# One weight unit of an expert layer is loaded in two transfers, and a scatter waits for four stores without a memset before it

## The chip, the cores and the metric

One Trainium2 chip, one of its cores. The metric is the device time of one launch in microseconds (us). The kernel before took 933.2 us, the median of three runs (932.6 to 933.7).

## The reference

One layer of a bidirectional encoder over 512 tokens of width 1024: three attention branches in parallel, their gated sum, a layer norm, an expert-choice mixture of 16 experts, and a second layer norm. The change lies in the last two steps. Cut to what matters there:

```python
aff = softmax(x @ w_router)
gate, idx = top_k(aff.T, 64)                     # each of 16 experts takes 64 tokens
h = einsum('becd,edf->becf', x[idx], w_gate_up)  # w_gate_up: 16 x 1024 x 2048
hg, hu = split(h, 2)
ye = einsum('becf,efd->becd', silu(hg) * hu, w_down) * gate
x = layer_norm(alpha * x + zeros.at[idx].add(ye))
```

## The kernel before, in words

Everything is float32. An expert's weights are cut into 12 units of 1 MB: eight of gate and up ("gu", e, k), 128 rows of 2048 numbers each, and four of down ("dn", e, k). All 192 units lie one behind the other in `in_wx`, in the order in which they are used. `_blocks` (line 50) lists the loads: pairs of units as one transfer of 2 MB, or single units of 1 MB at the start and at the end. `Ring.load` (line 885) issues the next one on SyncE's queue (line 920) into a ring of SBUF buffers; `Ring.done` calls it as soon as TensorE has read what lay in the buffer. Row r of a unit goes to partition r. A unit of 128 rows is spread over all 16 DMA engines, eight rows each.

TensorE works through the experts in order. `gate_up` (L1408) multiplies the 64 gathered tokens of an expert with a unit (16 matmuls, L1421), `act_h` makes the activation, `down` (L1467, L1475) multiplies it with the four down units one expert later. The results are added to the tokens' rows with one-hot matmuls (`combine`, L1558), between the units of later experts.

The last expert is dealt with apart. While its gate and up units run, the second layer norm is finished for all 512 rows without it, and four stores of 512 KB each (`norm_bias` L1638 for three, `norm_end` L1645 for the last) write the output on SyncE's queue, behind the last weights. `last_down` (L1672) then works out the 64 rows that the last expert touches anew: 128 matmuls of 128 columns (L1683), one quarter for each down unit, then statistics on VectorE (L1694 to L1697), the normalised rows `ul` (L1700, L1701), and an indirect DMA from GpSimd (L1703) that overwrites these rows in the output. It may not run before the four stores have landed. For that a memset of one number in each tile of `XO` (L1702) stands ahead of it on GpSimd: it writes the tile that the stores read, so it waits until they have landed, and the scatter comes behind it on the same engine.

Of the kernel before, what the change touches and what calls it, by code (L numbers as in the profile page):

```python
# [18 lines left out]
P = 128  # L19
# [15 lines left out]
N_SINGLE = 18  # L35
FULL = 43
EXTRA = ("gu", 1, 2)
X_SCALE = 1024.0
A_SCALE = 16384.0


def lead(e):
    return {NEXP - 2: 2, NEXP - 1: 1}.get(e, 4)
# [6 lines left out]
def _blocks():  # L50
    order = []
    for e in range(NEXP):
        order += [("gu", e, k) for k in range(lead(e))]
        if e:
            order += [("dn", e - 1, k) for k in range(4)]
        order += [("gu", e, k) for k in range(lead(e), KD)]
    order += [("dn", NEXP - 1, k) for k in range(4)]
    order.remove(EXTRA)
    blocks, i, r = [], 0, 0
    while i < len(order):  # L60
        for tag, n in RING:
            left = ROUNDS.get(tag, len(order)) - r
            if left > 0 and i < len(order):
                keys = order[i:i + n]
                i += n
                if r and (i < FULL or i > len(order) - N_SINGLE):
                    blocks += [(tag, h, [key]) for h, key in enumerate(keys)]
                else:
                    blocks.append((tag, 0, keys))
        if r == 0:  # L70
            tags = [t for t, _, _ in blocks]
            blocks.insert(tags.index("M"), ("Z", 0, [EXTRA]))
            blocks.insert(tags.index("raw") + 1, ("X", 0, order[i:i + 1]))
            i += 1
        r += 1
    return blocks
# [3 lines left out]
def layer_kernel(ctx: ExitStack, tc: tile.TileContext, xt, xn, first0, wu, bgate, rpb, gains, wrt,  # L80
                 lnp, lnt, wx, csn, nmask, tri, iota, out, dbg=None):
    nc = tc.nc
# [218 lines left out]
    gT = cp.tile([P, KD], F32, name="gT")  # L301
    nc.gpsimd.tensor_scalar(gT, lnT[:, 0], 1.0 / X_SCALE, None, op0=ALU.mult)

# [573 lines left out]
    class Ring:  # L877
# [7 lines left out]
        def load(self):  # L885
            tag, h, keys = self.blocks[self.n]
            n = len(keys)
            src = wx[self.row:self.row + P * n].rearrange("(p j) (h c) -> p (j h) c", j=n, h=2)
            if tag == "X":
                key, = keys  # L890
                spare["bf"] = R("bf", [P, 768], "wxa")
                g = [spare["bf"][:, :512], R("tmp", [P, 512], "wxb", bufs=2)]
                u = R("gb", [P, D], "wxc")
                nc.sync.dma_start(u, src[:, 1])
                nc.sync.dma_start(g[1], src[:, 0, 512:])
                nc.sync.dma_start(g[0], src[:, 0, :512])
                self.t[key] = [g, u]
                self.at[key] = (tag, 0)
                self.row += P
                self.n += 1  # L900
                return
            if tag == "Z":
                key, = keys
                spare["xs"] = R("hi", [P, 2, KD, 2 * CAP], "xs")
                g = spare["xs"][:, 1].rearrange("p k c -> p (k c)")
                u = [spare["bf"][:, 512:], small([P, 5 * CAP], "same", bufs=1)[:, :256],
                     spare["x1T"].rearrange("p a s -> p (a s)")]
                nc.sync.dma_start(g, src[:, 0])
                nc.sync.dma_start(u[0], src[:, 1, :256])
                nc.sync.dma_start(u[1], src[:, 1, 256:512])  # L910
                nc.sync.dma_start(u[2], src[:, 1, 512:])
                self.t[key] = [g, [u[:2], u[2]]]
                self.at[key] = (tag, 0)
                self.row += P
                self.n += 1
                return
            if tag not in self.home:
                self.home[tag] = R(tag, [P, 2 * dict(RING)[tag], D], f"w{self.n}")
            full = self.home[tag][:, 2 * h:2 * (h + n)]
            nc.sync.dma_start(full, src)  # L920
            for j, key in enumerate(keys):
                t = [full[:, 2 * j + i] for i in range(2)]
                if key[0] == "dn" and key[1] == NEXP - 1:
                    t = [x.rearrange("p (c n) -> p c n", c=4) for x in t]
                self.t[key] = t
                self.at[key] = (tag, h + j)
                self.busy.add((tag, h + j))
            self.row += P * n
            self.n += 1
# [254 lines left out]
    def norm_cols(ms):  # L1184
        c = slice(ms[0], ms[-1] + 1)
        nc.gpsimd.tensor_scalar(r13[:, c], rs_y[:, c], X_SCALE, None, op0=ALU.mult)
        for m in ms:
# [358 lines left out]
    def residual_rows(h):  # L1546
        g, b = (ln_row(i, h, f"r1{i}{h}")[:, None, :].to_broadcast([P, 2, 512]) for i in range(2))
        for mp in range(2):
            a = acc_half(mp, h)
            nc.vector.scalar_tensor_tensor(a, a, DN_ALPHA / X_SCALE, g, op0=ALU.mult, op1=ALU.mult)  # L1550
        for mp in range(2):
# [58 lines left out]
        for o in range(2):  # L1610
            nc.vector.tensor_copy(idx[o * 64:o * 64 + 64], ix[o * 64:o * 64 + 64, o:o + 1])

    XO = []

    def norm_mean(m):
        if m == 0:
            XO.append(R(ring.free_at_end.pop(0), [P, NT, D], "xo"))
        c = slice(m, m + 1)
        nc.gpsimd.tensor_scalar(l2_n[:, c], l2_s[:, m, 0:1], l2_s[:, m, 1:2], -1.0 / D, op0=ALU.add, op1=ALU.mult)
        nc.scalar.activation(XO[0][:, m], acc_of(m), AF.Square, bias=l2_n[:, c], accum_out=l2_q[:, c])  # L1620

# [5 lines left out]
    def norm_gain(m):  # L1627
        for o in range(2):
            c = slice(o * 512, o * 512 + 512)
            nc.vector.scalar_tensor_tensor(XO[0][:, m, c], acc_of(m)[:, c], l2_n[:, m:m + 1], LATE["g"][o], op0=ALU.add,  # L1630
                                           op1=ALU.mult)

    def norm_scale(m):
        nc.scalar.activation(XO[0][:, m], XO[0][:, m], AF.Copy, scale=l2_y[:, m:m + 1])

    def norm_bias(m):
        nc.gpsimd.tensor_tensor(XO[0][:, m], XO[0][:, m], LATE["b"], op=ALU.add)
        nc.sync.dma_start(out[:, m], XO[0][:, m])  # L1638

    def norm_end(m):  # L1640
        for o in range(2):
            c = slice(o * 512, o * 512 + 512)
            nc.vector.scalar_tensor_tensor(XO[0][:, m, c], XO[0][:, m, c], l2_y[:, m:m + 1], LATE["b"][:, c], op0=ALU.mult,
                                           op1=ALU.add)
        nc.sync.dma_start(out[:, m], XO[0][:, m])  # L1645

    def last_rows(zb):
        for m in range(NT):
# [23 lines left out]
    def last_down(zb, h, banks):  # L1672
        st = LATE["sl"]
        hT = R("bf", [P, 4, P], "hTl")
        w = {}

        def part(q, i):
            if q not in w:
                w[q] = [x[:, c] for x in ring.get("dn", NEXP - 1, q) for c in range(4)]
            for j in range(4 * i, 4 * i + 4):  # L1680
                c, hf = divmod(j, 2)
                for o in range(2):
                    nc.tensor.matmul(zb[o * 64:o * 64 + 64, q * P:(q + 1) * P], hT[:, c, hf * 64:hf * 64 + 64],  # L1683
                                     w[q][4 * hf + c][:, o * P:(o + 1) * P], start=False, stop=(q == 3 and j == 7))
            if i:
                ring.done("dn", NEXP - 1, q)

        last_transpose(hT, h, 0, banks[0])
        last_own(zb, 1)
        part(0, 0)  # L1690
        last_transpose(hT, h, 1, banks[1])
        for q, i in ((1, 0), (0, 1), (1, 1), (2, 0), (2, 1), (3, 0), (3, 1)):
            part(q, i)
        nc.vector.bn_stats(st[:, 0], zb)  # L1694
        for i in (0, 64):
            nc.vector.tensor_tensor(st[64 - i:P - i, 1], st[i:i + 64, 0], st[i:i + 64, 2], op=ALU.add)
        nc.vector.bn_aggr(sl_mv, st[:, :2])  # L1697
        nc.gpsimd.tensor_tensor(sl_y, sl_mv[:, 1:2], power[:, :1], op=ALU.pow)
        u = R("t", [P, 512], "ul", bufs=2)
        nc.vector.scalar_tensor_tensor(u, zb, sl_mv[:, 0:1], LATE["gh"], op0=ALU.subtract, op1=ALU.mult)  # L1700
        nc.vector.scalar_tensor_tensor(u, u, sl_y, LATE["bh"], op0=ALU.mult, op1=ALU.add)  # L1701
        nc.gpsimd.memset(XO[0][:1, :, :1], 0.0)  # L1702
        nc.gpsimd.indirect_dma_start(out.rearrange("p m (o c) -> (p m o) c", o=2),  # L1703
                                     bass.IndirectOffsetOnAxis(ap=idx, axis=0), u, None)

    onehot(0, 0, 2)
    g0 = gather(0, 0, 2)
# [124 lines left out]
def _expert_rows(wgu, wdn):  # L1832
    import numpy as np
    dn = _down_slots(wdn)
    unit = {"gu": lambda e, k: wgu[e, k * P:(k + 1) * P], "dn": lambda e, k: dn[e, k]}
    return np.concatenate([np.stack([unit[t](e, k) for t, e, k in keys], 1).reshape(-1, 2048) for _, _, keys in _blocks()])


def _norm_rows(g1, b1, g2, b2):
# [106 lines left out]
```

## Time and profile before

| what | value |
|---|---|
| median of three runs | 933.2 us |
| the profiled execution | 932.51 us |
| its span, first to last instruction | 930.7 us |
| TensorE busy | 916.6 us (98%) |
| TensorE's granted clock, mean | 0.997 of full speed |
| moved by DMA | 251.41 MB |

The span is what the profile shows; 1.8 us of the profiled execution lie around it. A matmul's end is modelled, so TensorE's busy share does not say that it never waits: its waits are read from the weight loads (PEld), which stand one ahead of the matmuls. A "DMA share" of 1.0 means that all 16 DMA engines of the core are busy all the time.

### The profile page before, as it was taken

How to read it: one execution, taken by the hardware profiler on the slowest of the kernel's cores; microseconds unless marked ns; L12 is line 12 of the kernel's file. 1: busy time of each engine (PE TensorE's matmuls, PEld its weight loads, DVE VectorE, ACT ScalarE, POOL GpSimd, SP SyncE). 2: the span in 40 equal slices, each digit the busy share in tenths (PEclk: the TensorE clock that was granted, in tenths of full speed). 3: DMA queues.
4: the chain of work that ended last, by engine and by line, in shares of the span. 5: the costliest groups of instructions: out<-in, count | busy, mean ns of one | idle time of the engine just before them, and what ended most of it. 6: DMA issues, size and time to landing. Idle time of an engine off the chain costs nothing.

```text
span 930.7 us, 12821 instructions
## 1 busy us (share of the span) xinstructions
PE 916.6 (98%) x5216; PEld 591.5 (64%) x5216; DVE 438.9 (47%) x797; ACT 298.7 (32%) x568; POOL 90.3 (10%) x113
## 2 busy tenths in 40 slices
PE   9999999999999999999999999999999999999896
PEld 8898888888888888888776343444344334433334
DVE  6457958664476576338454112563232222331244
ACT  6345465665444454334232112111111111111022
POOL 0001304000122230100032000000000000000014
PEclk9999999999999999999999999999999999999998
DMA  9320221120432332566939999999999999999996
GB/s 366 124 92 23 91 73 64 46 90 25 119 99 102 106 85 69 193 260 247 413 123 406 426 429 430 430 428 431 431 429 431 430 431 430 431 431 428 427 425 290
DMA packets 40570, 251.41 MB, mean 270 GB/s; under 512 B 13168, under 2 KB 13808, under 8 KB 25536
## 3 DMA queue, kind: packets, MB, share of 16 engines
q1 hardware_dynamic: 40432, 250.34, 66.9%
q8 instruction: 41, 0.67, 0.3%
q0 software_dynamic: 80, 0.26, 0.1%
q14 instruction: 17, 0.14, 0.0%
HBM read 247.44 MB, written 2.36 MB: 268 GB/s over the span
## 4 chain that ended last, share of the span: by engine, by line
PE 87%; DMA 5%; DVE 4%; ACT 3%; issue 1%; POOL 0%; POOLq 0%; ACTq 0%; DVEq 0%; SPq 0%
PE g L1421 11%; PE u L1421 11%; PE y L1475 10%; PE gate L308 4%; PE gate L310 4%; PE gate L309 4%; DMA w<-in_wx 4%; PE ga L1378 3%; PE cb L1558 3%; PE pr L308 2%; PE pr L309 2%; PE pr L310 2%; PE nqk L310 2%; PE nqk L309 2%; PE nqk L308 2%; ACT att_twin L681 1%
## 5 line engine op out<-in xcount | busy, mean ns | idle before, releaser
L1421 PE MATMUL g<-w,xs 128*64 128x512 f32 x504 | 131.3, 599 | 1.3 <-DMA w<-in_wx 1.2
L1421 PE MATMUL u<-w,xs 128*64 128x512 f32 x504 | 129.5, 592 | 0.0
L1475 PE MATMUL y<-w,hT 128*64 128x512 f32 x480 | 106.0, 593 | 1.5 <-DMA w<-in_wx 1.2
L108 DVE TENSOR_TENSOR y<-y,y 64x512 fp32r<-64x512 f32 x30 | 20.7, 689 | 167.2 <-ACT y L107 167.2
L1421 PEld LDWEIGHTS u<-w,xs 128*64 128x64 f32 x504 | 36.2, 137 | 72.0 <-issue 71.1
L1475 PEld LDWEIGHTS y<-w,hT 128*64 128x64 f32 x480 | 34.2, 137 | 70.2 <-issue 65.4
L310 PE MATMUL gate<-xh,los 128*128 128x512 f32 x192 | 74.8, 389 | 0.0
L1421 PEld LDWEIGHTS g<-w,xs 128*64 128x64 f32 x504 | 32.9, 136 | 60.8 <-issue 54.6
L108 DVE TENSOR_TENSOR los<-raw_twin,his 128x1024 fp32r<-128x1024 f32 x38 | 50.6, 1336 | 39.4 <-ACT his L107 39.2
L107 ACT CAST y<-y 64x512 fp32r<-64x512 f32 x30 | 17.4, 579 | 141.5 <-PE y L1475 130.2
L308 PE MATMUL gate<-xh,his 128*128 128x512 f32 x144 | 56.9, 395 | 0.0
L309 PE MATMUL gate<-xl,his 128*128 128x512 f32 x144 | 56.1, 390 | 0.0
L1567 DVE TENSOR_TENSOR acc<-acc,cb 128x512 f32<-128x512 f32 x50 | 31.1, 682 | 37.7 <-PE cb L1558 37.7
L107 ACT CAST his<-raw_twin 128x1024 fp32r<-128x1024 f32 x39 | 40.8, 1046 | 5.3 <-PE wo L1213 2.0
L310 PEld LDWEIGHTS gate<-xh,los 128*128 128x128 f32 x192 | 36.0, 188 | 7.6
L1378 PEld LDWEIGHTS <-xhl 128*128 128x128 f16 x448 | 27.9, 98 | 8.0 <-issue 7.1
L681 ACT ACTIVATE att_twin<-gs,nm 128x512 f32<-128x512 f32 x32 | 21.7, 684 | 34.3 <-DVE nm L680 34.3
L1378 PE MATMUL ga<-oh,xhl 128*128 128x128 f16 (+1 forms) x448 | 30.6, 227 | 0.2
L308 PEld LDWEIGHTS gate<-xh,his 128*128 128x128 f32 x144 | 27.0, 188 | 5.8 <-DVE macc L556 0.2
L108 DVE TENSOR_TENSOR los<-raw_twin,los 128x1024 fp32r<-128x1024 f32 x20 | 25.3, 1263 | 11.4 <-ACT los L107 11.3
L309 PEld LDWEIGHTS gate<-xl,his 128*128 128x128 f32 x144 | 27.1, 188 | 5.3
L1465 ACT COPY hT<-ht 128x512 f32<-128x512 f32 x12 | 7.0, 586 | 72.6 <-PE ht L1460 72.6
(474 smaller groups left out, 1750.4 us busy)
## 6 DMA issues: line engine op xcount, KB each, us to landing
w<-in_wx SPq DMA_DIRECT2D x75, 2048.0 KB
w<-in_wx SPq DMA_DIRECT2D x40, 1024.0 KB
raw_twin<-in_wu SPq DMA_DIRECT2D x65, 512.0 KB
raw<-in_wu SPq DMA_DIRECT2D x8, 512.0 KB
xr<-in_xt SPq DMA_DIRECT2D x4, 512.0 KB
macc<-in_xn SPq DMA_DIRECT2D x2, 1024.0 KB
out<-xo SPq DMA_DIRECT2D x4, 512.0 KB
first<-in_first SPq DMA_DIRECT2D x4, 384.0 KB
```

The source lines that it names most:

```text
L107: nc.scalar.copy(hi, src)
L108: nc.vector.tensor_tensor(lo, src, hi.bitcast(F32), op=ALU.subtract)
L308: nc.tensor.matmul(acc, w_h, rh[:, k], start=(k == 0), stop=False)
L309: nc.tensor.matmul(acc, w_h, rl[:, k], start=False, stop=False)
L310: nc.tensor.matmul(acc, w_l, rh[:, k], start=False, stop=(k == nk - 1))
L681: nc.scalar.activation(self.p[:, h], self.s[h], AF.Exp, bias=nm[:, h:h + 1], accum_out=self.sm[:, h:h + 1])
L1378: nc.tensor.matmul(g, x[:, m, c], oh[:, m, sl], start=(m == 0 and x is XH), stop=(m == NT - 1 and x is XL))
L1421: nc.tensor.matmul(GU[e][b][hf * 64:hf * 64 + 64, c:c + n], xs, x, start=(k == 0), stop=(k == KD - 1))
L1465: nc.scalar.copy(homes[0][:, c], (tq if c.start else tp)[:, c])
L1475: nc.tensor.matmul(y[o * 64:o * 64 + 64], hT[:, c, hf * 64:hf * 64 + 64], w[j][:, o * 512:(o + 1) * 512], start=(k == 0 and j == 0), stop= ...
L1558: nc.tensor.matmul(cb, GT[pr][:, m], part[:, c], start=(n == 0), stop=(n == len(parts) - 1))
L1567: nc.vector.tensor_tensor(a, a, cb, op=ALU.add)
```

## The change

It takes one unit, ("gu", 6, 1), the second gate and up unit of expert 6, out of its pair, so that the block list has two loads of 1 MB there in place of one of 2 MB. The unit itself is loaded with two transfers: rows 0 to 79 as before, and rows 80 to 127 with a source of three dimensions, six groups of eight rows. For this the host lays those 48 rows out in another order, so that six groups are interleaved and can't be merged into one run. The destination of each row is the partition that it had before. The diff's own word for the number of groups is `LOW`, six; a transfer with an outer dimension of six is worked on by six DMA engines, eight rows each, and the transfer of 80 rows by sixteen, five rows each.

In the tail the memset goes, and the scatter gets a dependency on each of the four stores.

```diff
+APART = ("gu", 6, 1)
+LOW = 6
...
-                if r and (i < FULL or i > len(order) - N_SINGLE):
+                if r and (i < FULL or APART in keys or i > len(order) - N_SINGLE):
...
-            nc.sync.dma_start(full, src)
+            if keys == [APART]:
+                m = P - 8 * LOW
+                nc.sync.dma_start(full[:m].rearrange("p j c -> p (j c)"), wx[self.row:self.row + m])
+                nc.sync.dma_start(full[m:].rearrange("p j c -> p (j c)"),
+                                  wx[self.row + m:self.row + P].rearrange("(b a) c -> a b c", a=LOW))
+            else:
+                nc.sync.dma_start(full, src)
...
-        nc.sync.dma_start(out[:, m], XO[0][:, m])
+        STORES.append(nc.sync.dma_start(out[:, m], XO[0][:, m]))
...
-        nc.gpsimd.memset(XO[0][:1, :, :1], 0.0)
-        nc.gpsimd.indirect_dma_start(out.rearrange("p m (o c) -> (p m o) c", o=2),
+        put = nc.gpsimd.indirect_dma_start(out.rearrange("p m (o c) -> (p m o) c", o=2),
                                      bass.IndirectOffsetOnAxis(ap=idx, axis=0), u, None)
+        for x in STORES:
+            tc.add_manual_dep(put.ins, x.ins.name, mybir.DependencyInfo(mybir.DependencyClass.Sync, mybir.DependencyReason.DATA),
+                              reason="the same rows of the output")
...
+    rows = [np.stack([unit[t](e, k) for t, e, k in keys], 1).reshape(-1, 2048) for _, _, keys in _blocks()]
+    i = next(i for i, b in enumerate(_blocks()) if b[2] == [APART])
+    m = P - 8 * LOW
+    rows[i] = np.concatenate([rows[i][:m], rows[i][m:].reshape(LOW, 8, 2048).swapaxes(0, 1).reshape(-1, 2048)])
+    return np.concatenate(rows)
```

## Rows read from the trace of the kernel before

**Rows 1.** The page: the span, TensorE's busy share, DMA share in 40 slices.

```profile
span 930.7 us, 12821 instructions
...
PE   9999999999999999999999999999999999999896
...
DMA  9320221120432332566939999999999999999996
```

**Rows 2.** DMA view from 500 to 926 us: queue and kind, packets, MB, share of 16 engines.

```profile
DMA packets 16056, 181.33 MB, mean 426 GB/s; under 512 B 1803, under 2 KB 2046, under 8 KB 2720
...
q1 hardware_dynamic: 16032, 180.98, 99.8%
q8 instruction: 19, 0.31, 0.3%
```

**Rows 3.** Waits of PEld from 500 us on: total us, times, longest.

```profile
PEld g L1421 <- DMA w<-in_wx: 3.5, 5, 2.1
...
PEld y L1475 <- DMA w<-in_wx: 3.2, 3, 2.1
```

**Rows 4.** Timeline of PEld: a usual weight load, and those behind the waits.

```profile
862.94 0.14 PEld L1475 LDWEIGHTS y<-w,hT 128*64 128x64 f32 x2 [0.28 <-issue]
863.90 0.20 PEld L1475 LDWEIGHTS y<-w,hT 128*64 128x64 f32 x4 [0.82 <-DMA w<-in_wx]
...
868.74 0.20 PEld L1475 LDWEIGHTS y<-w,hT 128*64 128x64 f32 x4 [2.07 <-DMA w<-in_wx]
...
873.59 0.20 PEld L1421 LDWEIGHTS g<-w,xs 128*64 128x64 f32 x4 [2.08 <-DMA w<-in_wx]
...
910.88 0.24 PEld L1421 LDWEIGHTS g<-w,xs 128*64 128x64 f32 x4 [0.61 <-DMA w<-in_wx]
```

**Rows 5.** Chain of waits: the weight load and the last store in it.

```profile
837.56 35.99 DMA w<-in_wx
...
917.79 7.80 DMA out<-xo
925.58 0.02 issue
925.61 0.04 POOLq L1702
925.65 0.07 issue
925.72 0.09 POOL xo L1702
925.81 0.46 issue
926.27 1.47 POOLq L1941
```

**Rows 6.** Stretches of the tail: engines' busy time, PEclk, DMA share, GB/s (last three).

```profile
919.00:920.00 1.00, 1.00 (x22) 1.00 (x20) 0.00 (x0) 0.00 (x0) 0.00 (x0) 1.00 1.01 414
920.00:920.50 0.50, 0.50 (x14) 0.48 (x10) 0.00 (x0) 0.00 (x0) 0.00 (x0) 1.00 0.94 385
...
922.00:922.50 0.50, 0.50 (x12) 0.32 (x6) 0.00 (x0) 0.00 (x0) 0.00 (x0) 1.00 0.50 205
...
924.50:925.00 0.50, 0.00 (x0) 0.00 (x0) 0.40 (x2) 0.00 (x0) 0.05 (x1) 0.90 0.24 98
925.00:925.50 0.50, 0.00 (x0) 0.00 (x0) 0.50 (x1) 0.00 (x0) 0.00 (x0) 0.50 0.02 8
...
920.50:925.50 5.00, 2.06 (x37) 1.73 (x32) 2.66 (x6) 0.00 (x0) 0.55 (x1) 0.94 0.48 193
```

**Rows 7.** Stretches around the time of the unit's load.

```profile
610.00:620.00 10.00, 10.00 (x46) 3.85 (x42) 9.22 (x11) 0.60 (x1) 0.00 (x0) 1.00 1.02 433
620.00:630.00 10.00, 10.00 (x51) 4.45 (x52) 3.69 (x7) 1.17 (x2) 0.00 (x0) 1.00 1.00 428
630.00:640.00 10.00, 10.00 (x68) 4.16 (x65) 1.80 (x4) 1.62 (x3) 0.00 (x0) 1.00 1.00 428
```

**Rows 8.** Timeline of SyncE's queue: the loads issued from 608 us on, merged.

```profile
608.69 23.32 SPq L920 DMA_DIRECT2D w<-in_wx  x6
```

**Rows 9.** Line 920: duration of a load's issue on SyncE, min/median/max ns, count.

```profile
L920 SPq DMA_DIRECT2D w<-in_wx x115: 327/328/1392, 383.4 to 900.8; - x115
```

**Rows 10.** Timeline, all engines: the matmuls of the last down units and what follows.

```profile
916.13 6.43 PE L1683 MATMUL end<-w,hTl 128*64 128x128 f32 x112
...
922.61 0.70 DVE L1694 BATCH_NORM_STATS2 late<-end 128x6 f32<-128x512 f32 x1 [4.89 <-PE end L1683]
...
924.81 0.75 DVE L1701 SCALAR_TENSOR_TENSOR ul<-ul,sly,late 128x512 f32<-128x512 f32 x1
925.72 0.09 POOL L1702 MEMSET xo<- 1x4 f32 x1 [1.17 <-DMA out<-xo]
926.52 1.22 POOL L1703 DMA_INDIRECT out<-ul,idx  x1 [0.71 <-issue]
```

**Rows 11.** Stretches of two copies of 64 partitions each, lines 520 and 521.

```profile
237.50:238.00 0.50, 0.50 (x4) 0.42 (x3) 0.00 (x0) 0.50 (x1) 0.00 (x0) 1.00 1.05 430
...
238.50:239.00 0.50, 0.50 (x4) 0.42 (x3) 0.50 (x1) 0.00 (x0) 0.00 (x0) 1.00 1.09 221
239.00:239.50 0.50, 0.50 (x4) 0.42 (x3) 0.36 (x1) 0.00 (x0) 0.00 (x0) 1.00 0.88 197
```

More of the change, by code (lines that the diff above doesn't have):

```diff
@@ L1611, in slot_tables @@
             nc.vector.tensor_copy(idx[o * 64:o * 64 + 64], ix[o * 64:o * 64 + 64, o:o + 1])
-    XO = []
+    XO, STORES = [], []
     def norm_mean(m):
@@ L1644, in norm_end @@
                                            op1=ALU.add)
-        nc.sync.dma_start(out[:, m], XO[0][:, m])
+        STORES.append(nc.sync.dma_start(out[:, m], XO[0][:, m]))
     def last_rows(zb):
@@ L1835, in _expert_rows @@
     unit = {"gu": lambda e, k: wgu[e, k * P:(k + 1) * P], "dn": lambda e, k: dn[e, k]}
-    return np.concatenate([np.stack([unit[t](e, k) for t, e, k in keys], 1).reshape(-1, 2048) for _, _, keys in _blocks()])
+    rows = [np.stack([unit[t](e, k) for t, e, k in keys], 1).reshape(-1, 2048) for _, _, keys in _blocks()]
[3 more added lines that the diff above has]
+    return np.concatenate(rows)
 def _norm_rows(g1, b1, g2, b2):
```

## The prediction

> **What bounds the kernel now.** I began with the page's slices. TensorE is busy throughout, and from the 19th slice on so is DMA [rows 1]. The DMA view of that part alone says how full: 181.33 MB from 500 to 926 us at 426 GB/s, the sixteen engines taken up to 99.8% by loads and stores and to 0.3% by instruction fetches, 19 of them [rows 2]. So the mixture of experts runs at the speed of the weights, as long as TensorE waits for them. It does: PEld waits 3.5 and 3.2 us in all [rows 3], and the timeline puts the long waits late: 0.82 us before 863.90, 2.07 before 868.74, 2.08 before 873.59, 0.61 before 910.88, against 0.28 that a usual load idles [rows 4]. Up to 860 us TensorE lives off what the ring holds; behind that each unit's landing sets its pace. The chain agrees: the load that frees TensorE at 873.60 was issued 35.99 us earlier [rows 5], so SyncE is far ahead and only the queues' drain counts.
>
> A transfer has landed when the last of its engines has. The tail shows how unlike the engines are: the rate is 414 GB/s up to 920, then falls in steps to 205 at 922.00 and 98 at 924.50, and only in the half microsecond from 925.00 it is near nothing [rows 6]. No more loads are queued then, so each step is an engine running dry. The first is done about 920.2, the last about 925.0. From 920.5 to 925.5 the engines move 5.00 × 193 = 0.97 MB, which sixteen at 430 GB/s would move in 2.2 us [rows 6]. So the last engine ends some 2.5 us after a perfectly even split would (920.5 + 2.2 = 922.7 against about 925.2).
>
> **The change, part by part.** *The two transfers.* At 430 GB/s an engine moves 26.9 GB/s, and a row of 8 KB takes 8192 / 26.9 = 0.305 us. Before, each engine has eight rows of the unit. After, ten have five: 3 × 0.305 = 0.91 us less. Six have 5 + 8 = 13: 5 × 0.305 = 1.52 us more. The queue is never empty between this load and the end [rows 2, 7], so an engine keeps what it wins or loses. If the late engines are among the ten, each landing behind this unit comes 0.91 us earlier, provided the six have 0.91 + 1.52 = 2.4 us in hand against the last; the spread of about 5 us [rows 6] has room for it.
>
> Which engines are late no view names. But the packet records behind the views can be strung together by their times: the instruction fetches of rows 2 go round among eight engines, which lose time at each turn, and the other eight have none. The one load of eight rows (the norm rows, some 60 us ahead of this unit), if it takes the lowest engines, falls on six of those without fetches and on two with. That is what a change that loads the lowest six wants. It is an inference, and I treat it as one.
>
> What becomes of 0.91 us at the end? The three long waits and the one at 910.88 end with a landing; between 873.59 and 910.88 TensorE has no wait of its own to hide it in [rows 4]. The matmuls of the last down units run without a gap from 916.13 to 922.56 [rows 10], and what starts them depends on the activation that hangs on the unit of 910.88, so they move along. The stores stand in the same queues and move by the same 0.91 us. Both inputs of the scatter therefore come earlier: `ul` is ready at 924.81 + 0.75 = 925.56 [rows 10], the last store lands at 917.79 + 7.80 = 925.59 [rows 5]. That they meet within 0.03 us matters: earlier stores alone would be worth 0.03 us. Term: -0.91.
>
> SyncE issues three transfers in place of one: 2 × 0.33 = 0.66 us [rows 9], at 608.69 us (the pair is the 71st load from the end [rows 8]). Behind them the next loads stand, with DMA share at 1.00 to 1.02 [rows 7], so the queue does not notice. Two loads of 1 MB for one of 2 MB moves the first a little earlier, into the same full queue. Zero, while the queue lasts.
>
> *The scatter.* The chain is: store landed 925.58, semaphore 925.61 to 925.65, 0.07 to the memset, memset 0.09 to 925.81, then 0.71 until the indirect DMA at 926.52 [rows 5, 10]. The memset and its start go: 0.07 + 0.09 = 0.16 us. The 0.71 has no releaser; the scatter's start-up may well need it whoever is ahead, so I keep it. Bounds: nothing (the new waits cost as much as the memset) and 0.16 + 0.71 = 0.87 (it all belonged to the memset). I take 0.16, since the only thing that the rows show to go is the memset. Behind the scatter GpSimd has only the program's end, so the waits hold nobody up. Term: -0.16.
>
> *Sum.* 932.51 - 0.91 - 0.16 = 931.44 for the profiled execution; that one lay 0.69 below the median, so 933.2 - 1.07 = 932.1 us.
>
> **The rivals.** *Shared partitions: slower.* Two copies that write 64 partitions each run at 430 GB/s for their first half microsecond and then at 221 and 197 [rows 11], with all engines busy. Sixteen engines on half of the partitions move half as much, so there is a limit on the side of the partitions too. The six groups go to partitions 80 to 127, and other engines are writing there at full rate. If a row of theirs costs a home engine 0.305 us, eight rows cost it 2.44 us; less the 0.91 it saves, the late engine ends 1.53 later, and 933.2 + 1.53 - 0.16 = 934.6 us. If the 80 rows on sixteen engines also lie across their homes, five rows at half rate add up to 1.52: 936.1. It decides if these visited engines are the late ones, or become so. For it: rows 11, the only case of the kind. Against: those copies have SBUF on both sides, and none of them is a load. [...]
>
> *Nothing from the transfers.* If the partitions' side is the limit but loses no time in all, each partition still gets the same rows, and the late ones end when they did. Then only the scatter gains: 933.2 - 0.16 = 933.0 us. The same comes out if TensorE's path, not the landings, holds `ul` where it is. For it: rows 11 again; against it: the waits in rows 4 are on landings.
>
> *The late engines are among the six.* Then they carry 1.52 us more: 933.2 + 1.52 - 0.16 = 934.6. Only if my reading of the packets is wrong.
>
> *The scatter gets it all.* With the full 0.87 the forecast becomes 933.2 - 0.91 - 0.87 = 931.4 us.
>
> **How the numbers follow.** Forecast 0.52 (of which 0.12 with the whole 0.71 or most of it), nothing from the transfers 0.18, shared partitions 0.25, late engines among the six 0.05. The likeliest gives 932.1, with its own range 931.2 to 932.8 (0.87 for the scatter and the 0.2 us or so between runs at the low end, a third of the 0.91 only at the high end). Against no change a measurement of this kernel can tell about 0.2%, 1.9 us: faster means under 931.3, slower over 935.1. The forecast falls inside; only with the scatter's whole bound, 931.4, it stands at the border, and I give most of that case's 0.12 to faster, 0.10. Shared partitions at 934.6 is inside too, at 936.1 out: slower gets 0.15 of its 0.25 and 0.01 of the engines' case, 0.16 together. The rest, 0.74, is the same. The range that leaves out 0.2 goes from 931.2 to 935.3: it holds all of the forecast, the second and fourth cases and the lower half of the shared partitions.
>
> **What the profile after would show.** Right: the waits before 863.9, 868.7 and 873.6 end about 0.9 us earlier; the rate in the tail falls more steeply, with the last step near 924.1 and not 925.0; `ul` and the last store both near 924.7; no memset, and the scatter some 0.8 us behind the store's landing (0.94 before), or at once if the bound holds. Shared partitions: DMA share stays at 1.0 but the rate around 615 to 630 us falls under 428 GB/s for some microseconds, the tail is longer, and the waits from 863 us on are longer. Nothing from the transfers: tail and waits as in rows 4 and 6. What would make the prediction wrong: an idle queue between 610 us and the end, or a new wait of TensorE at expert 6.

## The result, and the profile after

The kernel with the change takes 938.15 us (median of 6 runs, 937.37 to 939.82) against 932.93 us before (932.57 to 933.7): a ratio of 1.0058, 95% interval 1.0045 to 1.0071. It is slower by 5.2 us, and outside the predicted range. The profiled execution took 938.04 us, its span 936.3 us; TensorE's granted clock is 0.998 of full speed, as before.

The page of the kernel after, its span and its slices of 23.4 us (the last line is the rate of DMA):

```profile
span 936.3 us, 12824 instructions
...
DMA  9320321120532332566939999999999999999996
GB/s 366 122 94 27 97 77 47 49 88 23 140 108 75 101 85 85 229 249 248 407 131 413 426 427 431 430 329 429 431 429 431 429 430 430 430 430 430 426 425 286
```

DMA is as busy as before [rows 1], but one slice in the long plateau moves 329 GB/s where its neighbours move 430: the 27th, 609 to 632 us. The stretches of 5 us around it (the last three columns are PEclk, DMA share and GB/s), which answer to [rows 7]:

```profile
600.00:605.00 5.00, 5.00 (x26) 1.63 (x24) 2.20 (x2) 0.00 (x0) 0.00 (x0) 1.00 1.02 436
605.00:610.00 5.00, 5.00 (x24) 1.64 (x22) 2.17 (x3) 1.16 (x2) 0.00 (x0) 1.00 1.01 429
610.00:615.00 5.00, 5.00 (x26) 1.70 (x24) 4.97 (x5) 0.60 (x1) 0.00 (x0) 1.00 0.99 419
615.00:620.00 5.00, 5.00 (x24) 2.21 (x22) 4.25 (x7) 0.00 (x0) 0.00 (x0) 1.00 1.01 269
620.00:625.00 5.00, 5.00 (x28) 2.67 (x26) 3.17 (x6) 1.17 (x2) 0.00 (x0) 1.00 1.06 184
625.00:630.00 5.00, 5.00 (x26) 1.72 (x24) 0.10 (x1) 0.00 (x0) 0.00 (x0) 1.00 1.00 372
630.00:635.00 5.00, 5.00 (x26) 1.67 (x24) 0.75 (x2) 1.16 (x2) 0.00 (x0) 1.00 1.01 433
```

The DMA share stays at 1.0 throughout, so no engine is idle: each packet takes longer. (The trace also records every packet, behind the views. A row of 8 KB takes 0.309 us where nothing disturbs it; of the 256 rows of this unit and the next one, 210 take over 0.36 us, the median of these 0.67. The pages count 13168 packets under 512 B before and 13190 after: 22 more, all of 4 bytes, for two transfers more. From 600 to 640 us of the kernel before there are 128 of them beside 1048 rows, about sixteen to a load of 128 rows; so the 22 fit sixteen engines on one transfer and six on the other.) From 615 to 630 us the engines move 5 × (269 + 184 + 372) = 4.1 MB where 431 GB/s would have moved 6.5. Over 612 to 632 us the mean is 312 GB/s, before it was 431: a deficit of 20 × (431 - 312) / 431 = 5.5 us of queue time. That accounts for the loss (5.2 us in the medians, 938.04 - 932.51 = 5.5 us between the two profiled executions), and behind it the rate is the old one. I use this reckoning for every experiment below and call it *the deficit*; it is always that of the one execution that was profiled.

PEld's waits from 500 us on (us in total, times, longest), against 3.5 and 3.2 us in [rows 3]:

```profile
PEld g L1429 <- DMA w<-in_wx: 8.6, 7, 2.1
...
PEld y L1483 <- DMA w<-in_wx: 7.7, 6, 2.1
```

and PEld's timeline behind the dip, to be read against [rows 4]:

```profile
761.57 0.20 PEld L1483 LDWEIGHTS y<-w,hT 128*64 128x64 f32 x4 [1.23 <-DMA w<-in_wx]
...
766.42 0.20 PEld L1429 LDWEIGHTS g<-w,xs 128*64 128x64 f32 x4 [2.08 <-DMA w<-in_wx]
...
771.28 0.20 PEld L1429 LDWEIGHTS g<-w,xs 128*64 128x64 f32 x4 [2.09 <-DMA w<-in_wx]
```

The first wait for a landing that is longer than the usual 0.28 us comes at 761 us, a hundred us before the first one of the kernel before and 130 us behind the dip. TensorE did not notice the dip when it came: the ring's stock hid it, and was smaller from then on. At the end each landing is late by 6.1 us, a little more than the queue had lost: the weight loads at 863.90 and 868.74 [rows 4] come at 869.96 and 874.81.

The end of the chain of waits (start, us, what), against [rows 5]:

```profile
843.20 36.44 DMA w<-in_wx
...
923.89 7.35 DMA out<-xo
...
931.86 1.47 POOLq L1955
```

and the timeline of the last steps, against [rows 10]:

```profile
928.61 0.70 DVE L1702 BATCH_NORM_STATS2 late<-end 128x6 f32<-128x512 f32 x1 [4.78 <-PE end L1691]
...
930.81 0.75 DVE L1709 SCALAR_TENSOR_TENSOR ul<-ul,sly,late 128x512 f32<-128x512 f32 x1
932.11 1.22 POOL L1710 DMA_INDIRECT out<-ul,idx  x1 [1.57 <-DVE ul L1709]
```

The last store lands at 923.89 + 7.35 = 931.24, 5.65 us later than before (925.59), and the scatter starts 0.87 us behind it (0.94 with the memset). So the scatter's part is worth a few hundredths, and the loss is all there when the stores land. The other input, `ul`, is ready at 930.81 + 0.75 = 931.56, 6.0 us later than before (925.56) and 0.32 us behind the store; the profile puts the scatter's wait down to it, because it came last.

### The profile page after: what moved, and what is told of

It reads as the page before. It is cut to its first block, busy times and chain, and to the rows that moved or that the text cites. A ratio compares the mean times of both kernels' runs of the same rounds, so it can differ in the third digit from the quotient of the medians.

```text
span 936.3 us, 12824 instructions
## 1 busy us (share of the span) xinstructions
PE 917.4 (98%) x5216; PEld 590.3 (63%) x5216; DVE 438.8 (47%) x797; ACT 298.9 (32%) x568; POOL 90.2 (10%) x112
## 2 busy tenths in 40 slices
DMA packets 40720, 251.41 MB, mean 269 GB/s; under 512 B 13190, under 2 KB 13830, under 8 KB 25558
## 4 chain that ended last, share of the span: by engine, by line
PE 79%; DMA 13%; DVE 4%; ACT 3%; issue 1%; POOL 0%; SPq 0%; POOLq 0%; ACTq 0%; DVEq 0%
DMA w<-in_wx 12%; PE g L1429 9%; PE u L1429 9%; PE y L1483 7%; PE gate L310 4%; PE gate L312 4%; PE gate L311 4%; PE ga L1386 3%; PE cb L1566 2%; PE pr L310 2%; PE pr L311 2%; PE pr L312 2%; PE nqk L312 2%; PE nqk L311 2%; PE nqk L310 2%; ACT att_twin L683 1%
```

## The experiments

In all of them the unit ("gu", 6, 1) stands by itself in the block list, as in the change (but e1), and the scatter is that of before (but e1). `full` is the unit's place in the ring. The diffs are cut: `p j c -> p (j c)` on the left side and the host's new order of the rows are left out, and numbers stand for `m` and `LOW`. "Rate" is that of 612 to 632 us, and with the deficit it is that of the profiled execution; the time is the median, and single executions of e6 and e7 lie between 936.2 and 941.2 us.

| run | us | ratio, 95% interval | rate, GB/s | deficit, us |
|---|---|---|---|---|
| e1 scatter alone | 932.93 | 0.9999, 0.9990 to 1.0008 | 431 | 0 |
| e2 transfers alone | 938.92 | 1.0063, 1.0048 to 1.0079 | 310 | 5.6 |
| e3 80 + 48 rows | 935.89 | 1.0038, 1.0027 to 1.0049 | 361 | 3.2 |
| e4 two column halves | 933.19 | 1.0006, 0.9997 to 1.0016 | 426 | 0.2 |
| e5 sixteen groups of eight | 936.45 | 1.0039, 1.0024 to 1.0054 | 358 | 3.4 |
| e6 eight engines, low half | 938.15 | 1.0055, 1.0036 to 1.0074 | 331 | 4.6 |
| e7 eight engines, high half | 938.53 | 1.0057, 1.0037 to 1.0076 | 343 | 4.1 |
| e8 the change's transfers, two units | 948.56 | 1.0155, 1.0135 to 1.0176 | 285 | 6.8, and a second dip |
| e9 rows 32 to 95 first | 935.00 | 1.0028, 1.0017 to 1.0038 | 380 | 2.4 |
| e10 rows 0 to 63 first | 935.61 | 1.0029, 1.0018 to 1.0040 | 355 | 3.5 |
| e11 eight times sixteen rows | 936.46 | 1.0041, 1.0028 to 1.0055 | 355 | 3.5 |
| e12 the same, every eighth | 936.28 | 1.0045, 1.0031 to 1.0058 | 348 | 3.9 |
| e13 four half units, from 32 | 928.65 | 0.9957, 0.9944 to 0.9971 | 431 | 0 |
| e14 four half units, from 0 | 938.87 | 1.0068, 1.0054 to 1.0081 | 386 | 2.1 at the first |

The kernel before took 932.4 to 932.9 us beside them.

### e1 and e2: one part at a time

```diff
-        nc.gpsimd.memset(XO[0][:1, :, :1], 0.0)
...
+        for x in STORES:
+            tc.add_manual_dep(put.ins, x.ins.name, mybir.DependencyInfo(mybir.DependencyClass.Sync, mybir.DependencyReason.DATA),
+                              reason="the same rows of the output")
```

> The tail's part of the change alone: the scatter waits for the four stores, no memset; the unit is loaded as before. If the whole loss of 5.2 us comes from the two transfers, this kernel is at 932.1 to 933.0 us (0.0 to 0.87 us under the kernel before, most likely 0.16 under), with the scatter some 0.78 us behind the last store's landing (0.94 before). If instead the new waits on GpSimd cost the time, it is near 938 us.

```diff
-            nc.sync.dma_start(full, src)
+                nc.sync.dma_start(full[:80], wx[self.row:self.row + 80])
+                nc.sync.dma_start(full[80:], wx[self.row + 80:self.row + P].rearrange("(b a) c -> a b c", a=6))
```

> The two transfers alone (80 rows on sixteen engines, six groups of eight on six), memset kept. If they carry the loss: 938.1 to 938.6 us, the rate at 615 to 627 us falls to about 200 GB/s with the DMA share still at 1, and every landing behind is about 5 to 6 us later. If the two parts only cost together: between 933 and 936 us.

e1 stays at 932.93 us and e2 takes 938.92: the whole loss is in the two transfers. e1 alone, its end of the chain and its scatter:

```profile
918.08 8.09 DMA out<-xo
...
926.83 1.47 POOLq L1943
```

The store lands at 926.17. The timeline of GpSimd there:

```profile
924.60 0.55 POOL L1698 TENSOR_TENSOR sly<-slmv,power 128x1 f32<-128x1 f32 x1 [7.79 <-DVE slmv L1697]
...
927.08 1.22 POOL L1702 DMA_INDIRECT out<-ul,idx  x1 [1.94 <-DVE ul L1701]
```

The scatter starts 0.91 us behind the landing with nothing between them; here `ul` is ready at 925.41 + 0.75 = 926.16, together with the store. Most of what lay behind the memset [rows 5] was the scatter's own start, and it now stands behind the store's landing instead.

### e3 and e4: is it the rebalancing, or that there are two transfers?

```diff
+                for r in (slice(0, 80), slice(80, P)):
+                    nc.sync.dma_start(full[r], wx[self.row + r.start:self.row + r.stop])
```

> The same cut at row 80, but both transfers on all sixteen engines (five rows and three rows each), source in the old order; memset kept. Nothing is rebalanced. Theory shared partitions (an engine that writes outside its usual partitions shares their way in with the engine that writes there): still slow, by 1.8 to 3.5 us, 934.7 to 936.4, with a dip of the rate at 615 to 625 us; the 80 rows fill 64 partitions of the lower half first, which have half of the ways in. Rival, six engines with 13 rows become the last: no loss, 932.6 to 933.3 us, no dip. Rival, rows strided in memory or an outer dimension of six are slow: no loss either.

```diff
+                for j in range(2):
+                    nc.sync.dma_start(full[:, j], src[:, j])
```

> The unit is again alone and in two transfers, but cut by columns: 128 rows of 1024 columns each, twice, so that every engine keeps its rows and its partitions. Theory shared partitions: no loss, 932.6 to 933.3 us, no dip. Rival, two transfers in place of one (one more issue, packets of half the size, more semaphores in flight) cost the time: as slow as the change or at least 1 us slower.

e3 gives every engine 5 + 3 = 8 rows, as before, from a plain source, and loses 3.0 us. e4 has two transfers too, each of 128 partitions with half the columns, and loses nothing that can be told (0.3 us). So the uneven shares are not needed for the loss, and a second transfer alone does not bring it; a cut across the partitions is enough. With the six groups (e2) it is 6.0 us, twice that of e3. The groups change both the shares and which engine writes which partition, and this pair can't tell the two apart; together they cost 3 us more than the even cut.

### e5 to e7: which engine writes which partition

```diff
+PARTS = [(0, 128, 16)]
...
+                for lo, hi, g in PARTS:
+                    x = wx[self.row + lo:self.row + hi]
+                    if g:
+                        x = x.rearrange("(b a) c -> a b c", a=g)
+                    nc.sync.dma_start(full[lo:hi], x)
```

> The unit in one transfer again, 128 rows, all sixteen engines with eight rows each; only the source is laid out as sixteen groups of eight, as the change does it with six, so that an engine should get eight neighbouring rows. Memset kept. Same bytes, same engines, same partitions, no rebalancing, no second transfer. Theory shared partitions (what counts is which engine writes which partition): a dip of the rate and a loss of 2 to 3 us, 935 to 936 us. Rival, a transfer that covers fewer than 128 partitions is what costs: no loss, 932.6 to 933.3. Rival, six engines are overloaded: no loss. Should a plain transfer give each engine eight neighbours anyway, this changes nothing and there is no loss either.

e5 has one transfer of 128 rows, eight rows on each of sixteen engines: what should differ is which rows an engine has (eight partitions in a row) and the order in which it reads them. It loses 3.6 us, more than I had forecast. In e6 and e7 half of the unit is moved in two transfers of eight groups of four, the low half or the high half; both were meant for the same eight engines, which no view names:

```diff
+PARTS = [(0, 32, 8), (32, 64, 8), (64, 128, 0)]
```

> Three transfers: rows 0 to 31 and rows 32 to 63 as eight groups of four each (eight engines, four rows each), then rows 64 to 127 plainly on sixteen engines (four rows each). Eight engines carry 12 rows, eight carry 4. Memset kept. [...] To be read beside the next run, which has the same three shapes on the other halves. Rival, overloaded engines or few engines per transfer: the same time in both.

```diff
+PARTS = [(64, 96, 8), (96, 128, 8), (0, 64, 0)]
```

> The same three shapes with the halves exchanged: rows 64 to 95 and 96 to 127 as eight groups of four on eight engines, then rows 0 to 63 plainly on sixteen. Memset kept. [...]

The totals can't be told apart, 938.15 and 938.53 us with several us between single executions: the forecast difference, a loss of 1 to 2.4 us in e6 and of 2.4 to 4 in e7, did not come, and they lose 5.3 and 5.7 us. Only the beginning agrees with it. The stretches of e6 from 616 us on (columns as above):

```profile
616.00:618.00 2.00, 2.00 (x12) 0.57 (x8) 1.89 (x3) 0.00 (x0) 0.00 (x0) 1.00 1.00 393
...
622.00:624.00 2.00, 2.00 (x12) 1.59 (x11) 0.65 (x2) 0.59 (x1) 0.00 (x0) 1.00 1.03 180
624.00:626.00 2.00, 2.00 (x14) 0.94 (x14) 1.83 (x4) 0.59 (x1) 0.00 (x0) 1.00 0.98 193
```

and those of e7:

```profile
616.00:618.00 2.00, 2.00 (x11) 0.60 (x8) 1.85 (x3) 0.00 (x0) 0.00 (x0) 1.00 1.09 295
...
622.00:624.00 2.00, 2.00 (x12) 1.55 (x10) 1.10 (x2) 0.59 (x1) 0.00 (x0) 1.00 0.99 233
624.00:626.00 2.00, 2.00 (x14) 0.85 (x14) 1.38 (x3) 0.59 (x1) 0.00 (x0) 1.00 1.05 324
```

The low half starts at 393 GB/s and the high half at 295, but later e6 is the slower one, 180 and 193 against 233 and 324. The difference had been worked out from an assumption of mine on which engines write which half, and no view shows that. By it e7 should hold more rows that are off their engines; that it costs no more speaks against a price by the row, or against the assumption.

### e8: the dose

```diff
+APART = (("gu", 6, 1), ("gu", 10, 1))
```

> The two transfers of the change for two units, (gu, 6, 1) and (gu, 10, 1), memset kept. Theory: the queue is never empty, so what the DMA engines lose at each unit is kept to the end: a second dip of about 10 us near 730 to 750 us, and twice the loss, 942 to 945 us. Rival, the loss at expert 6 is one of order (semaphores or buffers out of step once): near 938.9, as with one unit. Rival, the second unit evens out engines that the first has made late: between 939 and 941.

Two units lose 15.7 us, where one loses 6.0 (e2), and 942 to 945 us were forecast. The second dip:

```profile
740.00:745.00 5.00, 4.84 (x24) 1.39 (x20) 1.38 (x2) 0.90 (x2) 0.00 (x0) 1.00 1.02 228
745.00:750.00 5.00, 2.43 (x12) 0.92 (x14) 0.67 (x1) 0.60 (x1) 0.00 (x0) 1.00 1.01 197
750.00:755.00 5.00, 1.23 (x6) 0.14 (x2) 0.76 (x2) 0.00 (x0) 0.00 (x0) 1.00 1.00 211
755.00:760.00 5.00, 3.85 (x12) 1.37 (x14) 0.00 (x0) 0.00 (x0) 0.00 (x0) 0.66 0.99 423
```

Three whole stretches are at half rate: the deficit here is 5 × (203 + 234 + 220) / 431 = 7.6 us. Now the stock no longer covers it: TensorE (second column) is busy 1.23 of 5 us, and its granted clock is 0.66 in the stretch after (1.00 in those before). The two dips make 14.4 of the 15.7 us. I had taken the price of a unit as fixed, and it is not: the same two transfers cost 5.6 us of queue in e2 and 6.8 and 7.6 in e8. Why, no run shows.

### e9 to e12: which partitions a transfer reaches

The forecasts of these four, and of e13 and e14, rest on an assumption of mine: that certain partitions belong to an engine, and that an engine which writes elsewhere shares the rate there. Which engine writes which row no view names, so the pairing itself was not shown.

```diff
+PARTS = [(32, 96, 16), (0, 32, 0), (96, 128, 0)]
```

> Three transfers on sixteen engines: rows 32 to 95 as sixteen groups of four, then rows 0 to 31 and 96 to 127 plain. [...] Loss about half of that of the sixteen groups of eight: 1.3 to 2.2 us, 934.1 to 935.0 us, 375 to 405 GB/s over 612 to 632 us, and its dip starts over 1 us later than in the other kernel of this pair. If the grouped (strided) reading of the source, or a transfer of fewer than 128 rows as such, costs the time: the same time as the other kernel within 0.5 us.

```diff
+PARTS = [(0, 64, 16), (64, 96, 0), (96, 128, 0)]
```

> The same three sizes and the same grouping of the source, but the 64 grouped rows are rows 0 to 63, then rows 64 to 95 and 96 to 127 plain. [...] Loss 3 to 4 us, 935.8 to 936.8 us, 350 to 370 GB/s over 612 to 632 us: at least 1 us above the other kernel. By the rival the two are equal within 0.5 us.

The rates, 380 and 355 GB/s, lie inside their forecasts (375 to 405 and 350 to 370). But the medians differ by 0.6 us where at least 1 was forecast, the ratios not at all (1.0028 and 1.0029), and the dip, which was to start over 1 us later in e9, starts at 617 us in both: the pair does not decide. The next pair differs only in which partitions each of eight small transfers reaches. The forecasts were 937.2 to 940.8 us and 265 to 335 GB/s for e11, and 935.1 to 936.7 us and 350 to 385 GB/s for e12 (its diff is against e11):

```diff
+                for r in range(8):
+                    nc.sync.dma_start(full[16 * r:16 * r + 16], wx[self.row + 16 * r:self.row + 16 * r + 16])
```

> The unit in eight transfers of sixteen rows, one row for each engine, source addresses in order; transfer r writes partitions 16r to 16r + 15. [...] If what costs is only that a transfer is short of 128 partitions, or the number of transfers, whatever the partitions: the same time as the other kernel of this pair within 0.5 us.

```diff
-                    nc.sync.dma_start(full[16 * r:16 * r + 16], wx[self.row + 16 * r:self.row + 16 * r + 16])
+                    nc.sync.dma_start(full[r::8], wx[self.row + 16 * r:self.row + 16 * r + 16])
```

> The same eight transfers of sixteen rows, the same source addresses, one row for each engine; but transfer r writes the partitions r, 8 + r, 16 + r and so on, every eighth one (the host lays the unit's rows out for it). [...] By the rival the two are equal within 0.5 us.

936.46 and 936.28 us: equal, which is what the rival said, and e11 misses its forecast. The price that I had put on how a transfer's partitions are spread fell. Part of it is that the small transfers also leave engines idle; the worst stretch of e12 (DMA share before the rate):

```profile
620.00:622.00 2.00, 2.00 (x11) 0.62 (x11) 1.14 (x2) 0.00 (x0) 0.00 (x0) 1.00 0.46 139
```

Over 612 to 632 us the share is 0.95 in e12 and 0.97 in e11, against 1.00 or 1.01 in the other runs: 1.0 and 0.6 us of the 20, which the pair was not built to keep apart. After it I could not say whether the partitions counted at all, or only the shape of a transfer. Hence the last pair.

### e13 and e14: the same transfer, 32 partitions further down

```diff
+APART = (("gu", 6, 1), ("gu", 8, 1), ("gu", 10, 1), ("gu", 12, 1))
+FIRST = 32
...
+                x = wx[self.row:self.row + 64].rearrange("(b a) c -> a b c", a=16)
+                nc.sync.dma_start(full[FIRST:FIRST + 64], x)
```

> Of four units (experts 6, 8, 10 and 12, second gate and up unit) only 64 rows are loaded, each unit in one transfer of sixteen groups of four, to partitions 32 to 95; the other 64 rows of these units are left out. [...] If the grouped source or a transfer of fewer than 128 rows as such is slow: a dip in the rate, the same time as the other kernel within 1 us, 932 to 936 us.

```diff
-FIRST = 32
+FIRST = 0
```

> [...] By the theory half rate or worse: each unit wins 1.22 us for the rows left out and loses 1.22 to 1.8 us, so 932.5 to 935.2 us, a dip at each of the four, 390 to 408 GB/s in 612 to 632 us, and at least 3.5 us above the other kernel. If the partitions do not matter: equal to it within 1 us.

Both kernels leave out half of the rows of these four units, so they are worth comparing with each other alone. One number differs: e14 writes the rows to partitions 0 to 63. They are 10.2 us apart: 928.65 us, inside its forecast of 927.3 to 929.5 (no dip, and for four units four rows of an engine less each, 4 × 4 × 0.305 = 4.9 us of queue), and 938.87 us, 3.7 us beyond its own. The page's slices of e13, by rate:

```profile
GB/s 367 126 92 23 91 74 64 46 87 29 120 92 105 112 86 68 183 272 230 408 116 408 426 430 428 430 430 430 429 429 431 430 430 429 431 429 432 424 427 271
```

and those of e14:

```profile
GB/s 361 127 91 23 93 78 55 45 90 24 135 107 80 102 85 73 229 247 256 404 128 409 426 429 429 431 392 430 408 408 430 371 430 430 386 431 430 426 426 290
```

e13 has none of the four dips; e14 has them all (392, 408 and 408 on a slice's edge, 371, 386). Over 20 us each (from 612, 670, 732 and 790 us) e14 moves 386, 377, 362 and 377 GB/s; at 431 that is a deficit of 2.1, 2.5, 3.2 and 2.5 us, 10.3 in all, which is the whole difference of the pair. In stretches of 2 us around the first unit, e13:

```profile
616.00:618.00 2.00, 2.00 (x11) 0.77 (x7) 1.45 (x3) 0.00 (x0) 0.00 (x0) 1.00 0.98 414
618.00:620.00 2.00, 2.00 (x11) 1.18 (x11) 1.80 (x4) 0.00 (x0) 0.00 (x0) 1.00 1.04 438
620.00:622.00 2.00, 2.00 (x13) 0.90 (x10) 0.68 (x2) 0.00 (x0) 0.00 (x0) 1.00 1.05 446
```

and e14:

```profile
616.00:618.00 2.00, 2.00 (x12) 0.57 (x8) 1.89 (x3) 0.00 (x0) 0.00 (x0) 1.00 1.11 389
618.00:620.00 2.00, 2.00 (x11) 1.31 (x8) 1.37 (x3) 0.00 (x0) 0.00 (x0) 1.00 0.92 201
620.00:622.00 2.00, 2.00 (x11) 0.60 (x9) 1.68 (x3) 0.00 (x0) 0.00 (x0) 1.00 0.96 238
```

So a transfer of 64 rows in sixteen groups from a strided source ran at full rate (414 to 446 GB/s) where its rows went to partitions 32 to 95, and at about half (201 to 238) where they went to 0 to 63. In this pair it is the partition that counts: neither a source in groups nor a transfer of fewer than 128 rows was slow as such. The packets say the same: of the 192 rows of the first such unit and the whole one behind it, every one took 0.309 us in e13, and 109 took over 0.36 us in e14, the median of these 0.59. e13 won 4.0 us of the 4.9 that its missing rows are worth, a little less because TensorE waits no more; PEld's waits from 500 us on:

```profile
PEld y L1481 <- DMA w<-in_wx: 0.6, 2, 0.3
...
PEld g L1427 <- DMA w<-in_wx: 0.3, 1, 0.3
```

No wait is longer than the usual 0.28 us or so: TensorE no longer waits for a landing, and by that further rows left out would win nothing, which no run tried.

## Why the prediction was wrong

**The bound: right.** What was lost in the queue at 620 us was lost at the end: a deficit of 5.5 us, and 5.2 us in the medians. In e1 to e5 and in the kernel after, deficit and loss agree within 0.4 us; in e14 the four deficits add up to its distance from e13.

**The two transfers: the step that failed.** I took a row as 0.305 us on whichever engine it lies ("At 430 GB/s an engine moves 26.9 GB/s, and a row of 8 KB takes 8192 / 26.9 = 0.305 us"), and so 0.91 us as won. The rate did not stay at 430 GB/s; it fell to 184 for 5 us, and the term of -0.91 became about +5.2. The rate went by which partitions were written: e13 against e14 shows that, 431 and 386 GB/s over 612 to 632 us. By themselves these two would also fit a rate that goes by the part of the partitions that one transfer reaches. e5 speaks against this: it reaches all 128 in one transfer of sixteen groups, at a DMA share of 1.01, and loses 3.6 us. What is left, an inference, is the pairing of engine and partitions; which engine wrote which row, no view names.

The rival *shared partitions*, at 0.25, had the direction and the marks: share at 1.0, rate under 428 GB/s between 615 and 630 us (269, 184 and 372), longer waits. Its price was the second error: 1.5 us for the eight rows of an engine and 1.5 more for the 80 rows. e3 puts the cut across partitions, even shares and all, at 3.0 us, and the six groups add some 2 to 3 (after and e2). I had let an engine lose only 0.305 us for each row that another one writes among its own. The pair of e13 and e14 shows 10.2 / 4 = 2.6 us a unit, and its packets show that more rows were slow than the 64 of the unit: 109, most of them at about half rate. So more rows were slowed than the reckoning has, rather than each row more; which engines they lay on, no view names. The row that should have warned me was in [rows 11]: 221 and 197 GB/s with all engines busy. I had it, and discounted it because those copies are within SBUF. (The 430 beside it I misread: 30 of the 45 packets of rows that start in that half microsecond are rows of 4 KB of another load, so it is not the rate of the copies alone.)

**SyncE: right.** The issue of the second transfer took 0.83 us and not 0.33, but the two transfers and the load behind them were issued by 608.6 us, ahead of the queue, and e4 with an extra transfer lies 0.3 us above the kernel before, within the noise.

**The late engines: not shown either way.** Which engines the six groups took no view names, and whether those have time in hand drowned in the loss. What can be said is that the six groups added loss (e2 against e3), by their shares or by their partitions.

**The scatter: -0.16 was too much.** Its wait behind the landing went from 0.94 to 0.87 (after) and 0.91 us (e1), and e1 stands at 932.93 against 932.88. The upper bound of 0.87 is excluded by these traces: most of the 0.71 us ahead of the scatter are its own. Even counted from `ul`, which is the later input in the kernel after, it starts only 932.11 - 931.56 = 0.55 us on.

**The other marks.** The tail is as long as it was: 181 GB/s over the 5 us from 926 us in which the queue drains, against 193 in [rows 6]. Inside it the rate falls sooner (49 GB/s from 929 to 930 us, over a us before the last store lands), but the last store is no earlier for it. The waits grew, but from 761 us on, and not from 863.

Open: why more rows are slow than the unit has (109 and 64 in e14, 210 and 128 in the kernel after), why the same transfers cost more in one place than in another (e8), and why e6 and e7, and e11 and e12, are alike. What limits the rate on the side of the partitions no run shows.

No version here beats the kernel before: e1 equals it, and e13 is faster only because it leaves rows out.

## What to carry to other kernels

Here a load of 128 partitions ran at full rate over 612 to 632 us, whole (431 GB/s) or cut by columns (426, e4), and one of 64 partitions too, where its rows were placed as in e13 (431). All the other cuts and placements across partitions lost 2 to 8 us a unit. Whoever cuts such a load across partitions, or hands rows to other engines, should measure the rate: here the rows and those queued behind them fell to half rate, 184 GB/s, while the engines showed as fully busy, a share of 1.06. Where a queue is the bound, look at GB/s in short stretches, since the DMA share did not show this loss; and a loss in a queue with stock in front of TensorE can show in the waits much later, here some 130 us.

## What the runs showed of the hardware

- Around a transfer of 64 rows in sixteen groups the rate was 414 to 446 GB/s at partitions 32 to 95 (e13), and fell to 201 to 238 at partitions 0 to 63 (e14), with nothing else changed.
- The dip outlasts the unit: 1 MB takes 2.4 us at 430 GB/s, but the rate of the kernel after is low from 615 to past 625 us (269, 184 and 372 GB/s in stretches of 5 us), and 210 rows of the unit and the one behind it were slow, 82 more than the unit has: the load queued behind it was slowed too.
- A full DMA share went with 184 GB/s (1.06, 620 to 625 us of the kernel after) as well as with 436 (1.02, 600 to 605 us).
- An indirect DMA on GpSimd started 0.87 to 0.94 us after the store that it waits for had landed, with a memset between (before) or without (e1, after).
